# Reordered weight loads, other places for quarter weights and pinned casts at the stage borders of a one-core encoder step

## The chip, the core and the metric

The kernel runs on one core of one Trainium2 chip. Its metric is the device time of one execution, in microseconds (us). Three runs of the kernel before took 946.75, 948.52 and 948.81 us, with a median of 948.52.

The core has a matrix engine (TensorE, PE in the profile; its weight loads are a row of their own, PEld), an elementwise engine (VectorE, DVE), an activation and copy engine (ScalarE, ACT), GpSimd (POOL) and a sequencer that here only issues transfers (SyncE, SP). Each works through its own list of instructions in order. Transfers are issued by SP, by POOL and a few by ACT; 16 DMA engines carry them.

## The reference, cut to what matters

One layer over 2048 prompt frames and 32 new frames, with 1024 channels, in float32:

```python
hn = rmsnorm(h, g_mix)
proj = hn @ w_in                                   # 1024 x 3072
hA, bA, cA, zA, vB, zB = jnp.split(proj, [...], axis=-1)      # six parts of 512
yA, new_conv = short_conv_mixer(hA, bA, cA, zA, conv_hist, conv_w, conv_b)
yB, new_pool = pooling_mixer(vB, zB, pool_hist, pos, pool_w, pool_scale)
h = h + jnp.concatenate([yA, yB], axis=-1) @ w_out             # 1024 x 1024
gate = jax.nn.sigmoid(rmsnorm(h, g_ple) @ w_ple_gate)          # 1024 x 1024
h = h + (p @ w_ple) * gate                                     # p is 256 wide
return rmsnorm(h, g_final)
```

The states of the convolution and of the pooling are outputs too.

## The kernel before, in words

**How a product is made.** Every float32 factor is split in two: ScalarE casts the tile to a rounded part (`nc.scalar.copy`, the "cast" of the profile), VectorE subtracts that from the tile and keeps the rest (the "lo"). A product of two split factors takes three matmuls for each block of 128 (`FINE`, line 100). The big products are not made as eight quarter products but as seven, in the manner of Strassen and Winograd: `11`, `12·21`, `S2·T2`, `S1·T1`, `S3·T3`, `S4·22`, `22·T4`, each of 12 matmuls of 128x512. The names are those of the combined quarters: of the frames `11, 12, 22, S1..S4`, of the weights `11, 21, 22, T1..T4` (in the first stage the roles are exchanged). `seven` (line 249) writes the order of one pair of frame tiles; `step(1)` to `step(6)` in it are points where other work is put in. In its `late` form, used by the output stage, the order is 11, step 1, half of S1·T1, step 2, S2·T2, step 3, the other half, step 4, S3·T3, step 5, 12·21, S4·22, step 6, 22·T4.

**Stage 1, the input projection** (lines 375 to 1262), runs over two groups of 1024 frames and, in each, over four column blocks j. A unit (`Unit.seven`, line 963) has three pairs of kinds: zb with v, c with h, za with b. The frame pieces of the second group were stored to memory and are fetched by `load_group` (line 532): seven pieces of 2 MB, issued by POOL. The raw weights of a pair are two loads of 512 KB (`raw_weight`, line 546), issued by SP from `pair_weights` (line 568) in rows of 512 bytes; they have three places. In the first unit of the second group the first two pairs go side by side and the third begins (its loads too) after step 6 of the second, order list at lines 1036 to 1040. Beside the pairs runs `aside`: in the last three units of the second group it takes one step of `turn_p` (p is turned and split), `new_frames` (line 1080, the 32 new frames; it loads them, takes their mean square, normalizes them, turns them by matmul with the identity) and `ple_weights`, one step after each step of a pair.

**Stage 2, the output product** (lines 1353 to 1440), first makes the embedding p·w_ple of seven tiles (`embed`, line 140; `EARLY` = 7): 12 matmuls of 128x512 for each tile into two banks, ScalarE copies each bank (line 167), POOL stores the tile. Then it runs `seven` over eight pairs of tiles. Beside the embedding, the weights of `w_out` are split: upper rows `tops` (`wo_t`), lower rows `bots` (`wo_b`), parts by `weight_parts` (line 200) and `weight_part` (line 188: a subtraction for T1..T4, a cast, a lo). There are three big places (`acts`, `slot`, line 335) and one smaller (`seventh`, line 342). The quarters `11, T1` and `T2, T3` have one big place each, the embedding's output the third, and `22, 21` take that one later (`place_last`, line 1401); `T4` has the smaller place, which until then holds the p of tiles 2 to 6 (line 1366, five loads of 256 KB). `LATER` (line 1405) says which quarters are made at which step of the first pair. In the first pair the carries are ScalarE copies (line 1284), later VectorE adds (line 1279).

**Stage 3, the gate** (lines 1443 to 1735), makes the other tiles of the embedding, with w_ple loaded to `shared` (line 1452, four loads of 512 KB), and then runs `seven` over eight pairs; `prep_g` (line 1658) loads, turns and splits the frames of the next pair at steps 2 and 3. Odd tiles are turned by VectorE from four loads (`turned_here`, line 1481), even ones by TensorE from one load (`turned`, line 1467). Here `T2, T3` have a big place, `21` and `T4` follow in the two halves of `shared`, `22` has the smaller one (lines 1701 to 1711).

**What sets the order.** The program order is not the order on an engine. When the program is built, a planner walks through it with estimated times and lists each engine's instructions by when it takes them to be ready, earlier ones of the program first; the chip then runs each list in that order. `tc.keep_in_program_order(ins)` pins an instruction among those of its engine, `tc.issue_after(ins)` puts a block's instructions behind another one on that engine. The planner also gives each tile the first place of its pool that is free by its reckoning, and an instruction that writes a place waits until the earlier user is done.

Of the kernel before, what the change touches and what calls it, by code (L numbers as in the profile page):

```python
# [9 lines left out]
F32 = mybir.dt.float32  # L10
# [26 lines left out]
def trunk(ctx, tc, x_p, x_s, c_conv, c_pool, p_p, p_s, g_mix, w_in, conv_w, conv_b, pool_w,  # L37
# [150 lines left out]
    def weight_part(W, q, k, top, bot, ready=False):  # L188
# [5 lines left out]
        if x is not None and not ready:  # L194
            nc.vector.tensor_tensor(t, x, y, op=ALU.subtract)
        hi, lo = W[q][0][:, k], W[q][1][:, k]
        nc.scalar.copy(hi, t)
        return nc.vector.tensor_tensor(lo, t, hi.bitcast(F32), op=ALU.subtract)

    def weight_parts(W, tops, bots, *names):  # L200

        for q in names:
            for k in range(KH):
                ins = weight_part(W, q, k, tops[k], bots[k] if bots else None)
        return ins

    def frame_parts(cmb, tmp, name, a11, a12, a21, a22, between=None):
# [167 lines left out]
    with ExitStack() as s1:  # L375
# [156 lines left out]
        def load_group(g):  # L532
            B = six(g)
            B["T4"] = piece_of(seventh(f"B{g}_T4"), 0)
            for q in NAMES:
                nc.gpsimd.dma_start(B[q].bitcast(F32), p_d[q])
            return B
# [8 lines left out]
        def raw_weight(kind, j, name, ring=raw_ring):  # L546
            t = ring(f"raw_{name}")
            col = cols[kind] * WA + j * P
            raw_loads.append(nc.sync.dma_start(t, w_in[:, col:col + P].rearrange("(k p) n -> p k n", p=P)))
            return t  # L550

        raw_loads = []
# [527 lines left out]
        def new_frames():  # L1080
# [3 lines left out]
            yield  # L1084
            x = x_stat(x, True)
            yield
            normal(x)
            yield
# [175 lines left out]
    with ExitStack() as s2:  # L1264
# [44 lines left out]
        def prep_h(i, between=None):  # L1309
            lo, hi = load_y(i, 2 * P) if i else first_y  # L1310
            S[i], more = frame_parts(cmb, ss if i else None, f"y{i}", lo[:, :, :P], hi[:, :, :P], lo[:, :, P:], hi[:, :, P:],
                                     between)
# [33 lines left out]
        def rows_of_weight(pool, name, src, which):  # L1346
            a = []
            for k in range(KH):
# [15 lines left out]
        near = weight_seventh(W, "wo")  # L1364
        for i in range(2, EARLY):
            early_pps.append(load_pps(near[:, i * NH:i * NH + NH].rearrange("p (a k n) -> p a k n", a=2, k=2), i, nc.sync))
        bots, loaded = [], []

        def lower_rows():
            for k in reversed(range(KH)):  # L1370
                bots.insert(0, cmb.tile([P, D], F32, tag="c", name=f"wo_b_{k}"))
                last = (nc.sync if k < KH - 1 else nc.gpsimd).dma_start(bots[0], w_out[(KH + k) * P:(KH + k + 1) * P])
            loaded.append(last.ins)

        more = prep_h(0, lower_rows)
        weight_parts(W, tops, None, "11", "T1")
        weight_slot(W, "wo", *PLACES[1])
        space = acts[0].tile([P, SLOT], F32, tag="hn", name="eouts")
# [5 lines left out]
        for c in range(EARLY):  # L1384
            run(c)
# [3 lines left out]
        weight_parts(W, tops, bots, "T2")  # L1389
# [11 lines left out]
        def place_last():  # L1401
            weight_slot(W, "wo", *PLACES[2])
            later("21", 0)()

        LATER = {1: later("T3"), 2: place_last, 3: later("22", 1), 4: later("T4", 2)}
# [12 lines left out]
        for i in range(0, NT - 1, 2):  # L1418
# [19 lines left out]
            if i == 0:  # L1438
                next_gate()
                nc.sync.dma_start(g_bc, g_fin.partition_broadcast(P))  # L1440
# [8 lines left out]
        got = {c: load_pps(st.tile([P, 2, 2, P], F32R, tag="t", name=f"pps_{EARLY + c}"), EARLY + c, nc.sync) for c in range(2)}  # L1449
        for k in range(2):  # L1450
            for h in range(2):
                nc.sync.dma_start(wp[k][h].bitcast(F32), wl_d[k][h])
        bots, _ = rows_of_weight(cmb, "wg_b", g_d, 1)
# [27 lines left out]
        def turned_here(i):  # L1481
# [3 lines left out]
            for q in range(4):  # L1485
                nc.sync.dma_start(t[q * 32:q * 32 + 32].rearrange("p (g c) -> p g c", g=4),
                                  h_d[r:r + P, q * 256:q * 256 + 256].rearrange("(g p) c -> p g c", p=32))
            nc.vector.transpose(t, t)
# [169 lines left out]
        def prep_g(i):  # L1658
# [105 lines left out]
```

## Time and profile before

| What | Value |
|---|---|
| median of three runs | 948.52 us |
| the profiled execution | 950.14 us |
| its span, first to last instruction | 948.3 us |
| PE / PEld busy | 911.1 / 728.1 us |
| DVE / ACT / POOL busy | 696.5 / 457.4 / 150.3 us |
| mean granted clock of TensorE | 0.985 |
| moved by DMA | 199.57 MB, 210 GB/s over the span |

Stage 1 fills the span up to 545 us, stage 2 goes from there to 734 us, stage 3 to the end. A row of the timeline gives start, length, engine, line, operation, output and inputs, shape and count, and in brackets the idle time of the engine in front of it and what ended it. Since matmuls are pipelined, a row of 12 is shown some 0.16 us longer than the distance to the next row.

### The profile page before, as it was taken

The page shows a single profiled execution, that of the slowest core. Times are in us where ns is not written, and L with a number is a line of the kernel's source. Part 1 is how long each engine was busy: PE and PEld are TensorE (multiplying, and loading weights), DVE is VectorE, ACT ScalarE, POOL GpSimd, SP SyncE. Part 2 cuts the span into 40 slices and gives each one's busy share as a digit, 9 for nine tenths or more (in the row PEclk, how much of TensorE's full clock was granted, in tenths as well). Part 3 has the DMA queues.
Part 4 walks back from the last instruction along what each step waited for, and adds up shares of the span by engine and source line. Part 5 has one row for each costly group of instructions (what it writes and reads, how often), then busy time and mean ns, then how long its engine had stood idle before and what let it go on. Part 6 is the DMA issues. An engine that isn't in the chain of part 4 may idle for free. (4 is left out here: it accounts for less than half of the span.)

```text
span 948.3 us, 12212 instructions
## 1 busy us (share of the span) xinstructions
PE 911.1 (96%) x4186; PEld 728.1 (77%) x4186; DVE 696.5 (73%) x1148; ACT 457.4 (48%) x828; POOL 150.3 (16%) x291
## 2 busy tenths in 40 slices
PE   8999999999999899999999988999999999999996
PEld 6788887778887688666688866878887778877885
DVE  6995888797982597746677668855655858899884
ACT  7752554455443344423343356624435755565553
POOL 2200121122121014100010021211111301111112
PEclk9999999999999899999999999999999899999999
DMA  8165295756699556687652565876777794656563
GB/s 270 47 203 191 78 289 166 225 165 202 192 363 406 117 189 207 209 277 223 204 182 89 188 258 201 247 242 225 230 241 264 276 259 164 190 193 222 194 195 133
DMA packets 115099, 199.57 MB, mean 210 GB/s; under 512 B 13270, under 2 KB 72062, under 8 KB 114013
## 3 DMA queue, kind: packets, MB, share of 16 engines
q1 hardware_dynamic: 93181, 126.63, 42.9%
q0 software_dynamic: 19408, 67.77, 21.1%
q10 hardware_dynamic: 2448, 4.39, 1.3%
q8 instruction: 33, 0.54, 0.2%
q14 instruction: 29, 0.24, 0.1%
HBM read 133.06 MB, written 65.67 MB: 210 GB/s over the span
## 5 line engine op out<-in xcount | busy, mean ns | idle before, releaser
L185 PE MATMUL x_o<-wo_T,y_S 128*128 128x512 f32 x192 | 46.4, 391 | 2.9 <-ACT c_o L1284 2.9
L185 PE MATMUL z_g<-wg,g_S 128*128 128x512 f32 x192 | 48.5, 398 | 0.0
L185 PE MATMUL z_o<-wo,y_S 128*128 128x512 f32 x192 | 47.6, 390 | 0.0
L185 PE MATMUL x_g<-wg_T,g_S 128*128 128x512 f32 x192 | 46.9, 391 | 0.0
L185 PEld LDWEIGHTS x_o<-wo_T,y_S 128*128 128x128 f32 x192 | 35.9, 188 | 11.1 <-ACT c_o L1284 3.7
L185 PEld LDWEIGHTS z_g<-wg,g_S 128*128 128x128 f32 x192 | 36.4, 192 | 7.6 <-ACT c_g L1499 0.2
L185 PEld LDWEIGHTS x_g<-wg_T,g_S 128*128 128x128 f32 x192 | 36.2, 188 | 7.6
L615 PE MATMUL z_ch<-B,w_ch_S 128*128 128x512 f32 x168 | 40.8, 392 | 1.2 <-ACT U L935 1.2
L185 PEld LDWEIGHTS z_o<-wo,y_S 128*128 128x128 f32 x192 | 36.0, 188 | 7.7 <-DVE y_S L84 0.3
L615 PE MATMUL x_ch<-B,w_ch_S 128*128 128x512 f32 x168 | 41.8, 392 | 0.0
L615 PE MATMUL x_zab<-B,w_zab_S 128*128 128x512 f32 x168 | 41.4, 394 | 0.4 <-ACT V L935 0.4
L615 PE MATMUL z_zab<-B,w_zab_S 128*128 128x512 f32 x168 | 41.7, 396 | 0.0
L615 PE MATMUL z_zbv<-B,w_zbv_S 128*128 128x512 f32 x168 | 41.5, 397 | 0.0
L615 PE MATMUL x_zbv<-B,w_zbv_S 128*128 128x512 f32 x168 | 40.6, 391 | 0.0
L615 PEld LDWEIGHTS z_ch<-B,w_ch_S 128*128 128x128 f32 x168 | 31.3, 188 | 8.9 <-ACT U L935 1.6
L615 PEld LDWEIGHTS z_zbv<-B,w_zbv_S 128*128 128x128 f32 x168 | 32.0, 192 | 7.5 <-issue 0.8
L615 PEld LDWEIGHTS x_zab<-B,w_zab_S 128*128 128x128 f32 x168 | 31.4, 189 | 8.4 <-issue 1.2
L615 PEld LDWEIGHTS z_zab<-B,w_zab_S 128*128 128x128 f32 x168 | 31.6, 190 | 7.4 <-issue 1.0
L615 PEld LDWEIGHTS x_zbv<-B,w_zbv_S 128*128 128x128 f32 x168 | 31.4, 188 | 7.3 <-issue 0.8
L615 PEld LDWEIGHTS x_ch<-B,w_ch_S 128*128 128x128 f32 x168 | 31.3, 188 | 7.3 <-issue 0.8
L1518 DVE SCALAR_TENSOR_TENSOR h<-h,rstd_f,g_bc 128x1024 f32<-128x1024 f32 (+1 forms) x15 | 19.2, 1283 | 15.4 <-POOL rstd_f L77 15.2
L81 ACT CAST y_S<-y_fS 128x512 fp32r<-128x512 f32 x28 | 17.1, 619 | 25.3 <-PE x_o L185 11.6
(562 smaller groups left out, 2303.0 us busy)
## 6 DMA issues: line engine op xcount, KB each, us to landing
wn<-in_w_in_dram SPq DMA_DIRECT2D x24, 512.0 KB, 4.8
p_dT<-T POOLq DMA_DIRECT2D x16, 512.0 KB, 5.1
y<-y_d SPq DMA_DIRECT2D x16, 512.0 KB, 4.5
h<-h_d SPq DMA_DIRECT2D x16, 512.0 KB, 5.8
e<-e_d SPq DMA_DIRECT2D x15, 512.0 KB, 4.7
x<-in_x_prompt_dram SPq DMA_DIRECT2D x14, 512.0 KB, 4.5
out_dram<-h POOLq DMA_DIRECT2D x14, 512.0 KB, 3.7
B<-p_d POOLq DMA_DIRECT2D x3, 2048.0 KB, 16.3
```

The lines of the kernel that those rows point to most:

```text
L81: ins = nc.scalar.copy(hi, src)
L185: nc.tensor.matmul(ps[:n], lhs[:, k, a, :n], w[b][:, k], start=start and k + q == 0, stop=k == KH - 1 and q == 2, skip_group_check=True)
L615: nc.tensor.matmul(ps, lhs[:, k, x], b[:, k, y], start=start and k + q == 0, stop=stop and k == KH - 1 and q == 2, skip_group_check=True)
L1518: nc.vector.scalar_tensor_tensor(h[:n], h[:n], rf[:n], g_bc[:n], op0=ALU.mult, op1=ALU.mult)
```

## The change

1. **Third pair of the second group's first unit.** `load_group` now also issues three raw weights, right behind its seven pieces: those of zb on SP, those of za and b on POOL. `raw_weight` hands them out when the pair asks for them.
2. **New frames.** `new_frames` has three more empty steps: one between load and mean square, one between that and the normalization, one behind it.
3. **Output weights.** The place of the embedding's output (`space`) is taken before that of `T2, T3`. The p of tiles 2 to 6 come by one load into the half place of T3. `21` has the smaller place, `22, T4` a big one. T2 is made ahead of the sixth tile of the embedding, in the row order 2, 1, 0, 3. The subtractions and casts of T2, T3, 21 and 22 are pinned. 21 and 22 are both made at step 2 of the first pair. Three lower rows of the weights are loaded behind the first split of the first frames, the fourth behind the second one.
4. **Final gain.** `g_bc` is loaded in the second pair (i = 2), not in the first.
5. **Gate weights.** One p tile instead of two and two lower rows instead of four are loaded ahead of w_ple, the other two rows behind it. `21, 22` have the big place, `T3` the smaller one, `T2` and `T4` the halves of `shared`.
6. **Gate frames.** The frames of the second gate pair are loaded ahead of h and e of the first, and that h is issued by POOL.

```diff
@@ weight_part, weight_parts @@
-        if x is not None and not ready:
-            nc.vector.tensor_tensor(t, x, y, op=ALU.subtract)
+        if x is not None and not ready:
+            ins = nc.vector.tensor_tensor(t, x, y, op=ALU.subtract)
+            if pin:
+                tc.keep_in_program_order(ins)
         hi, lo = W[q][0][:, k], W[q][1][:, k]
-        nc.scalar.copy(hi, t)
+        ins = nc.scalar.copy(hi, t)
+        if pin:
+            tc.keep_in_program_order(ins)
@@ frame_parts @@
             put("11", a11)
-            between()
+            between[0]()
             put("S3", comb("S3", a11, a21, ALU.subtract, a11))
+            between[1]()
@@ load_group, raw_weight @@
+            for kind, name, queue in (("zb", "zbv", nc.sync), ("za", "zab", nc.gpsimd), ("b", "zab", nc.gpsimd)):
+                name = f"{name}_{g}_0{'b' if kind == 'b' else 'a'}"
+                raw_ahead[name] = raw_weight(kind, 0, name, queue=queue)
...
+            if name in raw_ahead:
+                return raw_ahead.pop(name)
@@ stage 2 @@
-        near = weight_seventh(W, "wo")
-        for i in range(2, EARLY):
-            early_pps.append(load_pps(near[...], i, nc.sync))
+        space = acts[0].tile([P, SLOT], F32, tag="hn", name="eouts")
+        pair = weight_slot(W, "wo", *PLACES[1])[:, SLOT // 2:SLOT // 2 + (EARLY - 2) * NH]
+        with tc.issue_after(last_raw):
+            nc.sync.dma_start(pair.rearrange("p (i n) -> p i n", n=NH).bitcast(F32),
+                              pp_d[2:EARLY].rearrange("i p n -> p i n"))
...
+        W["21"] = halves(seventh("wo_21"))
...
         for c in range(EARLY):
+            if c == EARLY - 2:
+                weight_parts(W, tops, bots, "T2", order=(2, 1, 0, 3), pin=True)
             run(c)
...
-        weight_parts(W, tops, bots, "T2")
...
+        def third():
+            hold.append(weight_parts(W, tops, bots, "T3", pin=True))
+
+        def left():
+            weight_parts(W, tops, bots, "21", pin=True)
+            weight_slot(W, "wo", "22", "T4")
+            hold.append(weight_parts(W, tops, bots, "22", pin=True))
+            more(0)
+
+        LATER = {1: third, 2: left, 3: later(1), 4: later("T4", 2)}
@@ stage 3 @@
+        got = {0: load_pps(st.tile(...), EARLY, nc.sync)}
+        head, _ = rows_of_weight(cmb, "wg_b", g_d, 1, (0, 1))
         for k in range(2):
             for h in range(2):
-                nc.sync.dma_start(wp[k][h].bitcast(F32), wl_d[k][h])
+                last_q = nc.sync.dma_start(wp[k][h].bitcast(F32), wl_d[k][h])
-        bots, _ = rows_of_weight(cmb, "wg_b", g_d, 1)
+        bots = head
+        with tc.issue_after(last_q.ins):
+            bots += rows_of_weight(cmb, "wg_b", g_d, 1, (2, 3))[0]
...
+        W["T2"] = halves(shared)[2:]
+        weight_parts(W, tops, bots, "T2")
+        W["T3"] = halves(seventh("wg_T3"))
+        weight_parts(W, tops, bots, "T3")
+        weight_slot(W, "wg", "21", "22")
+        weight_parts(W, tops, bots, "21", "22")
...
-            h = [load_rows(xh, "h", i + b, h_d) for b in range(2)]
+            following = prep_g(i + 2, not i)
+            h = [load_rows(xh, "h", i + b, h_d, queue=nc.sync if i else nc.gpsimd) for b in range(2)]
```

More of the change, by code (lines that the diff above doesn't have):

```diff
@@ L1344, in scale_gate, with rows_of_weight @@
             return rest
-        def rows_of_weight(pool, name, src, which):
+        def rows_of_weight(pool, name, src, which, ks=range(KH)):
             a = []
-            for k in range(KH):
+            for k in ks:
                 a.append(ring4(pool, f"{name}_{k}") if pool is not cmb else cmb.tile([P, D], F32, tag="c", name=f"{name}_{k}"))
@@ L1439, in trunk @@
                 next_gate()
-                nc.sync.dma_start(g_bc, g_fin.partition_broadcast(P))
+            if i == 2:
+                with tc.issue_after(summed[-1].ins):
+                    nc.sync.dma_start(g_bc, g_fin.partition_broadcast(P))
         W = {}
@@ L1479, in turned, with by_quarters @@
             return out
-        def turned_here(i):
+        def by_quarters(i):
             r, n = tiles[i]
@@ L1672, in prep_g, with load @@
             lower = []
+            def load():
+                got["lower"] = by_quarters(i + 1)
+                got["upper"] = load_rows(ya, "hn", i, h_d) if i else first_h
+            if ahead:
+                load()
             def first():
-                lower.extend(turned_here(i + 1))
+                if not ahead:
+                    load()
+                lower.extend(turned_here(got["lower"]))
             def second():
```

61 lines of the change are left out of this document (28 added, 33 removed).

## The prediction

> **What bounds the kernel now.** I read the page's first part, then the waits of PE, then PE's timeline, and at each of its holes the timeline of the engine or queue that PE waited for.
>
> ```profile
> PE 911.1 (96%) x4186; PEld 728.1 (77%) x4186; DVE 696.5 (73%) x1148; ACT 457.4 (48%) x828; POOL 150.3 (16%) x291
> ...
> PE x_zab L615 <- ACT w_zab L81: 6.2, 1, 6.2
> PE e L109 <- ACT eouts L167: 3.5, 1, 3.5
> PE x_o L185 <- ACT c_o L1284: 2.9, 2, 2.2
> PE e L109 <- DMA wq<-wl_d: 2.7, 3, 1.5
> PE pth L1477 <- ACT ho L1475: 2.1, 1, 2.1
> PE pt_new L1092 <- DVE xt_new L453: 1.4, 1, 1.4
> PE x_o L185 <- DVE x L1279: 0.8, 1, 0.8
> ```
>
> PE is busy for 911.1 of 948.3 us. The change takes no matmul away, so it can only win in the 37.2 us in which PE stands, and in what a stop costs behind it. Seven rows of waits, 19.6 us in all, lie at the places that the diff touches. The waits are not the whole loss, since the clock falls in them:
>
> ```profile
> 312.70:322.20 9.50, 9.47 (x34) 7.65 (x35) 3.39 (x7) 1.13 (x2) 0.00 (x0) 0.79 0.81 180
> 396.70:408.00 11.30, 11.27 (x62) 6.96 (x62) 4.41 (x7) 2.09 (x4) 0.00 (x0) 0.85 0.87 264
> 780.40:786.00 5.60, 5.55 (x22) 4.64 (x23) 4.07 (x7) 3.35 (x6) 0.00 (x0) 0.70 0.45 139
> ```
>
> The third number from the end is the granted clock: 0.79, 0.85 and 0.70 behind waits of 6.2, 1.4 and 2.1 us. So I price each hole by distances in the timeline against a full rate, waits and slow matmuls together. The full rate comes from two rows that follow each other: 12 matmuls in 303.64 - 300.92 = 2.72 us, 0.2267 each.
>
> ```profile
> 300.92 2.88 PE L615 MATMUL x_zbv<-B,w_zbv_S 128*128 128x512 f32 x12
> 303.64 2.88 PE L615 MATMUL x_ch<-B,w_ch_S 128*128 128x512 f32 x12
> 312.73 2.50 PE L615 MATMUL x_zab<-B,w_zab 128*128 128x512 f32 x5 [6.21 <-ACT w_zab L81]
> 322.15 2.20 PE L615 MATMUL x_zbv<-B_T,w_zbv 128*128 128x512 f32 x9
> ```
>
> **1, the third pair.** PE was free at 303.64 + 2.72 = 306.36. Up to 322.15 it made 33 matmuls (5 and 4 of zab, two S4 products of 12), 7.48 us; lost: 8.3. PE's list held zab's first product in front of the two S4 products, and zab's raw weights were late:
>
> ```profile
> raw_zab_0b<-in_w_in_dram SPq DMA_DIRECT2D x1, 512.0 KB, 48.7
> raw_zbv_0b<-in_w_in_dram SPq DMA_DIRECT2D x1, 512.0 KB, 4.1
> B_T<-p_dT4b POOLq DMA_DIRECT2D x1, 2048.0 KB, 30.7
> 279.62 0.53 POOL L536 DMA_DIRECT2D B_T<-p_dT4b  x1 [1.67 <-PE x_zab L615]
> 312.06 1.14 ACT L81 CAST w_zab<-raw_zab_0a 128x512 fp32r<-128x512 f32 x2 [9.84 <-DMA raw_zab_0a<-in_w_in_dram]
> ```
>
> The same 512 KB take 4.1 us alone, but 48.7 us (the second) beside the seven pieces of the other queue, whose last lands at 279.62 + 30.7 = 310.3. Behind the pieces on POOL's queue, both raws land by 310.3 + 2 x 4.1 = 318.5 at the latest, the first by 314.4; at the earliest by some 306 and 308, as the pieces share with nothing. That helps PE little in itself: what counts is the list. The planner put zab first since it took the raws to be there before the last pieces; in one queue behind the last piece they can't be. So I expect both S4 and both 22 products first: 306.36 + 4 x 2.72 = 317.2 for zab's first product (first raw at 314.4 at worst, two casts of 0.6 us), and two products later, at 322.7, for the first that needs the second raw. Both bounds fit. What is late next is the last piece, wanted at 306.36 + 2 x 2.72 = 311.8 and there at 310.3 in before, so 1.5 us ahead. I take **7.3 of 8.3**; ends 8.3, and 0 if the list keeps its order. The three POOL issues and the one of SP stand in front of nothing that PE awaits: SP's raw of zb is issued early in before too, POOL's next loads (p) are for the next unit.
>
> The Trainium skill's "DMA: Bandwidth & Descriptors" (Issuing engines are not separate DMA queues) says that the issuing engine saves issue time only, the same 16 engines carrying all. By that rule the move to POOL would win nothing; the 4.1 against 48.7 speaks for the place in the queues.
>
> **2, the new frames.** A wait of 1.4 us, then 11.3 us at clock 0.85 (second window above): 1.4 + 0.15 x 11.3 = 3.1. Three empty steps of one product each give the chain of load, mean square, scale and transpose 8.2 us more, against a wait of 1.4; behind it only the same part's later steps move, and the three units have 72 steps where the parts take 49 and now 52. I take **2.5**; ends 0 (the planner puts the transposes as early as it did) and 3.1.
>
> **3, the output stage up to its first product.**
>
> ```profile
> 545.01 5.73 PE L109 MATMUL e<-wp,pps 128*128 128x512 f32 x24
> 569.58 2.88 PE L185 MATMUL x_o<-wo,y 128*128 128x512 f32 x12
> 560.54 0.69 DVE L195 TENSOR_TENSOR wo_t<-wo_b,wo_t 128x512 f32<-128x512 f32 x1 [5.88 <-DMA wo_b<-in_w_out_dram]
> 561.26 0.62 ACT L197 CAST wo_T<-wo_t 128x512 fp32r<-128x512 f32 x1 [5.95 <-DVE wo_t L195]
> wo_T<-pp_d SPq DMA_DIRECT2D x5, 256.0 KB, 3.1
> g_bc<-in_g_final_dram SPq DMA_DIRECT2D x1, 512.0 KB, 11.0
> 555.00:557.50 2.50, 2.50 (x13) 2.07 (x12) 0.00 (x0) 0.31 (x1) 0.00 (x0) 1.00 1.03 419
> ```
>
> 84 embedding matmuls from 545.01 are 19.04 us, to 564.05; the first product began at 569.58: 5.5 lost. The cause stands in three rows: a lower weight row landed at 560.5, VectorE's T2 waited for it, and ScalarE's T2 cast waited in front of the copies that PE needed to reuse its banks. Two parts of the change meet it. The pin keeps the T2 casts behind the copies of the first five tiles, so at 545.01 + 10 x 1.36 = 558.6 ScalarE has freed ten banks, and PE can go on over six banks, 8.2 us, without the next copy. And 5 x 256 KB of p go out before 545 (T3's place is free when the S4·22 product of the last pair has read it) and 512 KB of g_bc much later: 1.8 MB less at 419 GB/s, 4.3 us sooner for the rows. Either alone would do. I take the whole **5.5**, with 3 as the low end for an order of casts that I don't see.
>
> **4, the first output pair.**
>
> ```profile
> 593.68 2.43 PE L185 MATMUL x_o<-wo,y 128*128 128x512 f32 x10
> 577.35 3.22 ACT L197 CAST wo<-wo_b 128x512 fp32r<-128x512 f32 x6 [2.35 <-DMA e_d<-eouts]
> 580.48 0.57 ACT L1284 COPY c_o<-x_o 128x512 f32<-128x512 f32 x1
> ```
>
> From 569.58 to 593.68 PE made 86 matmuls (84 and 2 of the next pair), 19.5 us; lost: 4.6, most of it behind the copy c_o at 580.48, which stood behind six casts that had waited 2.35 us for a store of the embedding. In the change 21 needs no such store. But T3 can be cast only behind the last embedding product (564.05, as p lies in its place) and, pinned behind the first carry copy, from 564.05 + 2.72 + 0.57 = 567.4; with four casts each of T3, 21 and 22 at 3.22 / 6 = 0.54 us the queue of 12 ends at 573.8, and if the second carry stands behind it, at 574.4. S3·T3 wants that copy at 564.05 + 3 x 2.72 = 572.2. So one wait of 2.2 us stays where 4.6 was lost. VectorE also has less time to catch up. I take **1.7**; ends 4.6 (the copy is put ahead of 22) and -2.5 (22's casts still wait for the store, rival B).
>
> **5, the gate's embedding.**
>
> ```profile
> 731.34 2.88 PE L185 MATMUL x_o<-wo_T,y 128*128 128x512 f32 x12
> 753.90 1.03 PE L1477 MATMUL pth<-ident,ho 128*128 128x128 f32 x8
> 730.02 0.32 SPq L129 DMA_DIRECT2D pps<-pp_d  x1
> 730.46 2.01 SPq L1452 DMA_DIRECT2D wq<-wl_d  x4
> 723.18 2.88 PE L185 MATMUL x_o<-wo_T,y_S 128*128 128x512 f32 x12
> ```
>
> PE was free at 734.06; five tiles are 60 matmuls, 13.6 us, to 747.7; the transposes came at 753.90: 6.2 lost. The w_ple loads stood in SP's queue behind a p tile at 730.02, which is no longer in front. Their place is that of `T2, T3`, free after the product at 723.18 + 2.72 = 725.9, so they go out 4.5 us earlier, behind 1 MB less; the last wait ended at 738.6, and 4.5 less is 734.1, just when PE wants the first. I take **4.5**, a short wait being left; ends 2 and 6.2. The quarters behind it: 21 is wanted first and can now be made early; T2, wanted one product (2.72 us) later, takes over the place that frees last, so the order of needs is better than before.
>
> **6, the second gate pair's frames.**
>
> ```profile
> 775.70 2.65 PE L185 MATMUL x_g<-wg_T,g_S 128*128 128x512 f32 x11
> 785.97 2.88 PE L185 MATMUL x_g<-wg,g 128*128 128x512 f32 x12
> 769.02 1.97 SPq L1486 DMA_DIRECT2D hn<-h_d  x4
> 764.79 2.90 PE L185 MATMUL x_g<-wg,g 128*128 128x512 f32 x12
> ```
>
> 24 matmuls and 8 transposes (1.03) are 6.5 us; PE took 785.97 - 775.70 = 10.3: 3.8 lost. The frames' loads went out at 769.02, 4.2 us after the end of the embedding at 764.79. In the change they stand first, but their places are those of the upper weight rows, which T2 now holds until its lo: cast 0.6, lo 0.7, so from 766.2 on, 2.8 us sooner, and without h in front. The wait was 2.1, so it goes. e and h come later and can hold VectorE. I take **3.0**; ends 0 and 3.8.
>
> The Trainium skill's page "TensorE: Matmul & The Clock Gate" (What's actually happening) has the clock fall only after an idle window of about 3.4 us; by that rule 2, 5 and 6 could win their waits alone, 1.4, 2.7 and 2.1, and the sum would be 3.8 us smaller. The third window, clock 0.70 behind a wait of 2.1 us, disagrees, and the rows decide.
>
> **Sum:** 7.3 + 2.5 + 5.5 + 1.7 + 4.5 + 3.0 = 24.5 us. The profiled execution took 950.14 (span 948.3 and 1.84 around it), so 925.6 by it; it is 1.62 above the median of the runs shown, so the median comes to 948.52 - 24.5 = **924.0**.
>
> **Rivals.**
>
> A, the queue changes nothing for PE: the planner still lists zab's product first. For it: the list follows estimates that were 40 us wrong in before. Then PE waits from 306.36 for a raw at 308 to 314.4: as long as before, within some 4 us. 924.0 + 7.3 = **931**. Chance 0.17. (The rule of the Trainium skill's DMA page on issuing engines, cited above, points this way.)
>
> B, the pins hold the carry copies: 22's casts, pinned in front of the second carry, wait for the embedding's last store as those at 577.35 did, S3·T3 with them. Price: 2.5 lost instead of 1.7 won, **928**. Against it: copies and store come earlier, as ScalarE isn't blocked at 561. Chance 0.17.
>
> C, slower: VectorE's backlog of the first output pair never drains, and each of the seven later pairs waits as pair 2 of the gate does, 3.8 us: 924.0 + 7 x 3.8 = **951**. It decides from the point at which VectorE has more than the 19.04 us of a pair to do. Against it:
>
> ```profile
> 657.90:676.94 19.04, 19.04 (x86) 15.77 (x85) 10.75 (x17) 7.21 (x12) 4.32 (x8) 1.00 0.73 234
> ```
>
> VectorE is busy for 10.75 us of such a pair. Chance 0.07.
>
> **How the numbers follow.** The forecast has 0.56, with its own range 917 (all 31.5 us won) to 930. The 0.03 left lies between it and before. A and B together are 935.5, with 6's gain gone too 938.5: range 917 to 939. A measurement of this kernel can tell about 0.2% (1.9 us) from no change. Faster 0.56 + 0.17 + 0.17 = 0.90; same 0.03; slower 0.07.
>
> **What would show it.** 1: z_zbv follows S3·T3 without a hole at 306 and x_zab comes after the 22 products. 2: no wait of pt_new. 3: the first product of the output at 564 minus what was won before it, no wait of e for eouts. 4: one wait of x_o for c_o, about 2 us. 5: w_ple issued right behind the last S3·T3. 6: no wait of pth for ho. I would be wrong if a hole moves to the next late thing: the last frame piece, 22's casts, or e in the gate's first pair.

## The result and the profile after

The changed kernel took 938.75 us (median of four runs, 936.91 to 940.55), the kernel before 948.66 beside it (four runs, 946.75 to 950.83): ratio 0.9895, 95% interval 0.9861 to 0.9928, 9.9 us less. The forecast was 924.0, so of the 24.5 us it promised, 10 came. The profiled execution took 940.35 us with a span of 938.3, against 948.3 before. The first part of its page, busy times by engine:

```profile
PE 909.1 (97%) x4186; PEld 727.1 (77%) x4186; DVE 698.1 (74%) x1148; ACT 459.0 (49%) x828; POOL 149.7 (16%) x295
```

PE stands for 29.2 us now, 37.2 before. The waits of PE say where (total, times, longest):

```profile
PE x_o L185 <- ACT wo L199: 3.1, 1, 3.1
...
PE e L109 <- DMA wq<-wl_d: 2.0, 1, 2.0
PE pth L1506 <- ACT ho L1504: 2.0, 1, 2.0
...
PE x_zab L625 <- ACT w_zab_S L81: 1.4, 1, 1.4
...
PE z_zab L625 <- ACT w_zab_S L81: 0.8, 1, 0.8
```

Six of the seven old rows at the places of the change are gone from there; e for w_ple is still there with 2.0 us. New are the first, the third (in a later gate pair than before) and the last two. So holes were closed and others opened. Which counts most is read from distances between stages on PE's timeline, waits and slow clock together:

| Stretch of PE's timeline | before, us | after, us | won | forecast |
|---|---|---|---|---|
| start to first embedding product, parts 1 and 2 | 545.01 | 536.20 | 8.8 | 9.8 |
| embedding, to the first output product, part 3 | 24.57 | 19.16 | 5.4 | 5.5 |
| first two output pairs | 42.85 | 47.86 | **-5.0** | **1.7** |
| other output pairs, to PE free for the gate | 121.63 | 122.70 | -1.1 | 0 |
| embedding of the gate, part 5 | 30.73 | 28.59 | 2.1 | 4.5 |
| first gate pair (72 matmuls) with the next frames, part 6 | 21.18 | 17.29 | 3.9 | 3.0 |
| rest | 162.3 | 166.5 | **-4.2** | 0 |

The sum before rounding is 10.0, the difference of the spans. Three rows of seven are right; the output pairs miss 6.7 us, the rest of the gate 4.2, its embedding 2.4. Each column is one profile, and the runs below show how far a row moves from one to the next.

**The first output pair.** PE's timeline:

```profile
536.20 5.73 PE L109 MATMUL e<-wp,pps 128*128 128x512 f32 x24
...
555.36 2.88 PE L185 MATMUL x_o<-wo,y 128*128 128x512 f32 x12
...
566.78 0.50 PE L185 MATMUL x_o<-wo_T,y_S 128*128 128x512 f32 x1 [0.52 <-ACT wo_T L199]
...
577.66 8.13 PE L185 MATMUL x_o<-wo,y 128*128 128x512 f32 x22 [3.12 <-ACT wo L199]
```

The embedding runs without a hole now (19.16 us for 84 products). But the last product of the pair, 22·T4, waits 3.1 us for T4's cast, and the 22 matmuls in that row (12 of it, ten of the next pair) take 8.1 us where 22 x 0.2267 are 5.0: the third number from the end of the next row, the granted clock, is 0.62.

```profile
567.80:577.60 9.80, 6.60 (x27) 4.91 (x27) 9.80 (x18) 6.06 (x11) 0.00 (x0) 0.97 0.54 169
577.60:585.80 8.20, 8.13 (x22) 6.13 (x22) 4.94 (x9) 2.99 (x6) 2.70 (x6) 0.62 0.77 238
```

In the first of these windows VectorE (the third pair of numbers) is busy 9.80 us of 9.80. Why it was so late shows on its timeline from T2's first subtraction on:

```profile
550.67 0.68 DVE L195 TENSOR_TENSOR wo_t<-wo_b,wo_t 128x512 f32<-128x512 f32 x1
...
554.03 0.69 DVE L202 TENSOR_TENSOR wo_T<-wo_t,wo_T 128x512 fp32r<-128x512 f32 x1 [0.69 <-ACT wo_T L199]
554.63 0.69 DVE L195 TENSOR_TENSOR wo_t<-wo_b,wo_t 128x512 f32<-128x512 f32 x1
556.01 0.69 DVE L202 TENSOR_TENSOR wo_T<-wo_t,wo_T 128x512 fp32r<-128x512 f32 x1 [0.69 <-ACT wo_T L199]
...
567.20 0.68 DVE L202 TENSOR_TENSOR wo_T<-wo_t,wo_T 128x512 fp32r<-128x512 f32 x1
567.80 4.90 DVE L202 TENSOR_TENSOR wo<-wo_b,wo 128x512 fp32r<-128x512 f32 x8
```

and on ScalarE's:

```profile
561.72 0.62 ACT L199 CAST wo_T<-wo_t 128x512 fp32r<-128x512 f32 x1 [1.79 <-DVE wo_t L195]
...
566.63 4.26 ACT L199 CAST wo<-wo_b 128x512 fp32r<-128x512 f32 x8
...
576.95 0.62 ACT L199 CAST wo<-wo_b 128x512 fp32r<-128x512 f32 x1 [1.79 <-DVE wo_b L195]
```

Subtraction (L195), cast (L199), lo (L202), next subtraction: one part at a time, each engine waiting for the other. The eight parts of T2 and T3 take from 550.67 to 567.88, 17.2 us, 2.15 a part. Only then come 21, 22 and T4.

**The rest of the gate.** SyncE's queue in the third gate pair:

```profile
796.87 1.75 SPq L1515 DMA_DIRECT2D hn<-h_d  x4
804.30 0.34 SPq L377 DMA_DIRECT2D h<-h_d  x1
804.68 0.43 SPq L377 DMA_DIRECT2D hn<-h_d  x1
```

and ScalarE, for which PE's transposes then wait 2.0 us:

```profile
811.43 1.14 ACT L1504 COPY ho<-hn 128x512 f32<-128x512 f32 x2 [4.10 <-DMA hn<-h_d]
```

The frame row hn stands behind an h row that went out only at 804.30, when its place came free. In the kernel before both h rows of that pair had gone out together at 800.19, well ahead of the frames at 815.31, so hn had no waiting row in front of it.

**The third pair.** S4 and 22 come first, without a hole, as forecast. But what comes next on PE waits:

```profile
308.94 2.88 PE L625 MATMUL z_ch<-B,w_ch_S 128*128 128x512 f32 x12
...
317.10 2.88 PE L625 MATMUL x_zab<-B,w_zab 128*128 128x512 f32 x12
...
324.73 0.74 PE L625 MATMUL x_zab<-B,w_zab_S 128*128 128x512 f32 x2 [1.35 <-ACT w_zab_S L81]
326.30 0.73 PE L625 MATMUL z_zab<-B,w_zab_S 128*128 128x512 f32 x2 [0.83 <-ACT w_zab_S L81]
```

since VectorE takes S2's subtraction (the L587 row) behind operations of another chain, four of them 2.73 us in all:

```profile
320.09 2.73 DVE L1080 SCALAR_TENSOR_TENSOR c_s<-U,vec,c_s 128x512 f32<-128x512 f32 x4
322.75 0.68 DVE L1072 SCALAR_TENSOR_TENSOR pl<-win,V 128x512 f32<-128x512 f32 x1
323.35 0.68 DVE L587 TENSOR_TENSOR raw_zab_0a<-s_zab,raw_zab_0a 128x512 f32<-128x512 f32 x1
```

At the same number of matmuls PE is 8.45 us ahead of before at 314 us, and 5.7 us ahead at 328.

### The profile page after: what moved, and what is told of

Same layout as the page of the kernel before. It is cut to its first block, busy times and chain, and to the rows that moved or that the text cites. A ratio compares the mean times of both kernels' runs of the same rounds, so it can differ in the third digit from the quotient of the medians.

```text
span 938.3 us, 12210 instructions
## 1 busy us (share of the span) xinstructions
PE 909.1 (97%) x4186; PEld 727.1 (77%) x4186; DVE 698.1 (74%) x1148; ACT 459.0 (49%) x828; POOL 149.7 (16%) x295
## 4 chain that ended last, share of the span: by engine, by line
PE 64%; DVE 5%; DMA 5%; ACT 2%; issue 2%; POOL 1%; POOLq 0%; SPq 0%; DVEq 0%; ACTq 0%
PE x_g L185 8%; PE x_zab L625 7%; PE x_o L185 6%; PE x_ch L625 6%; PE x_zbv L625 5%; PE e L109 4%; PE z_g L185 4%; PE z_zab L625 4%; PE z_ch L625 3%; PE z_o L185 3%; PE z_zbv L625 2%; PE y_g L185 2%; PE y_zab L625 1%; PE y_o L185 1%; PE new L1124 1%
## 5 line engine op out<-in xcount | busy, mean ns | idle before, releaser
L185 PE MATMUL x_o<-wo,y 128*128 128x512 f32 x192 | 48.3, 407 | 3.1 <-ACT wo L199 3.1
L185 PEld LDWEIGHTS x_o<-wo,y 128*128 128x128 f32 x192 | 38.0, 199 | 11.9 <-ACT wo L199 3.5
L1551 DVE SCALAR_TENSOR_TENSOR h<-h,rstd_f,g_bc 128x1024 f32<-128x1024 f32 (+1 forms) x15 | 19.2, 1280 | 12.7 <-POOL rstd_f L77 12.0
```

The source lines that it names most:

```text
L185: nc.tensor.matmul(ps[:n], lhs[:, k, a, :n], w[b][:, k], start=start and k + q == 0, stop=k == KH - 1 and q == 2, skip_group_check=True)
L1551: nc.vector.scalar_tensor_tensor(h[:n], h[:n], rf[:n], g_bc[:n], op0=ALU.mult, op1=ALU.mult)
```

## The experiments

Theory T: the pins on subtraction *and* cast chain each part of T2 and T3 over two engines, and T4 is late. R1: not the pins, but that 22 is made ahead of T4. Q: the rest of the gate is lost to the order of one queue.

### No pins, cast pins, 22 later

Without pins:

```diff
-weight_parts(W, tops, bots, "T2", order=(2, 1, 0, 3), pin=True)
+weight_parts(W, tops, bots, "T2", order=(2, 1, 0, 3))
```

and so for T3, 21 and 22.

> The changed kernel with no pin on T2, T3, 21 and 22. Theory T (the pins chain subtraction, cast and lo of each part of T2 and T3, 2.0 to 2.3 us a part instead of about 1.45, so that T4's casts are 3.1 us late): VectorE makes the eight parts of T2 and T3 at about 1.4 us each, the wait of x_o for wo's cast in 22*T4 goes, and the first two output pairs (first product to first product of the third pair) fall from 47.9 to 42 to 45 us; the whole is 13 to 16 us under the kernel before instead of 9.9. A wait of x_o for the carry copy c_o of up to 2.2 us may come back, since nothing holds the casts behind it. Rival R1 (not the pins: 22 made ahead of T4 at step 2, in place of step 3): 47 to 49 us for the two pairs, 9 to 11 us under the kernel before.

Measured: 940.17 us, ratio 0.9921 (0.9893 to 0.9948), no faster than the changed kernel; the two pairs 46.6 us, the embedding 22.1 instead of 19.2. Its waits of PE:

```profile
PE x_o L185 <- ACT c_o L1297: 4.1, 2, 3.2
PE e L109 <- ACT eouts L167: 2.7, 1, 2.7
```

The chain is gone, but the planner again puts casts in front of the copies that free PE's banks, those of the embedding (2.7) and the carries (3.2). The pins on the casts do what the prediction said of them. So this run cannot settle T; the next one does. Only the casts pinned:

```diff
             ins = nc.vector.tensor_tensor(t, x, y, op=ALU.subtract)
-            if pin:
-                tc.keep_in_program_order(ins)
```

> The changed kernel with the casts pinned and the subtractions not. T: the chain is broken as well, since VectorE may run its subtractions ahead in threes; the two pairs take 42 to 45 us, within 1.5 us of the kernel without any pin. If the pinned casts alone were the cause: 47 to 49 us, as in the changed kernel. R1: 47 to 49 us.

Measured: 934.0 us, ratio 0.9857 (0.9837 to 0.9878); the two pairs **42.5** us instead of 47.9, the embedding 19.17 as in the changed kernel. VectorE's timeline:

```profile
551.94 1.89 DVE L195 TENSOR_TENSOR wo_t<-wo_b,wo_t 128x512 f32<-128x512 f32 x3
553.75 1.89 DVE L202 TENSOR_TENSOR wo_T<-wo_t,wo_T 128x512 fp32r<-128x512 f32 x3
555.55 1.90 DVE L195 TENSOR_TENSOR wo_t<-wo_b,wo_t 128x512 f32<-128x512 f32 x3
...
560.78 2.49 DVE L202 TENSOR_TENSOR wo_T<-wo_t,wo_T 128x512 fp32r<-128x512 f32 x4
```

Three subtractions run, then three lo's: T2 and T3 take 551.94 to 563.27, 11.3 us instead of 17.2. T is confirmed at its place. In time the median is 4.7 us under the changed kernel's 938.75, and 2.3 under the 936.32 that it took in a later set of runs; two more profiles with this edit, below, have 42.5 and 44.1 us in the two pairs. That the kernel without any pin would be as fast was wrong. A smaller wait is left, y_o for the frame part 12, whose cast now stands behind 22's:

```profile
566.94 0.74 PE L185 MATMUL y_o<-wo,y 128*128 128x512 f32 x2 [2.00 <-ACT y L81]
```

22 made at step 3, all pins kept:

```diff
-            hold.append(weight_parts(W, tops, bots, "22", pin=True))
             more(0)
+        def late_22():
+            hold.append(weight_parts(W, tops, bots, "22", pin=True))
+            more(1)
```

> The changed kernel, pins kept, with 22 made at step 3 as in the kernel before, and not at step 2. T: the chain of T2 and T3 is the same, so T4's casts stay late, and the two pairs take 46.5 to 49 us (47.9 in the changed kernel). R1: 42 to 45 us, and the wait of 22*T4 for the cast goes.

Measured: 935.31 us, ratio 0.9875 (0.9854 to 0.9895); the two pairs 46.0 us, between the two forecasts. The wait of 22·T4 is still there, now for a sum that stands behind T4's work on VectorE:

```profile
PE x_o L185 <- DVE x L1292: 3.8, 1, 3.8
```

So R1 holds for 1.9 of the 5.4 us at most: casts and lo's of 21 and 22 fill holes of the chain. Of the 1.9, 1.3 lie in the clock: the 22 matmuls behind the wait took 6.83 us here and 8.13 in the changed kernel. Most of the rest of this run's lead over the changed kernel lies in the gate's embedding (26.3 us for 28.6).

### The output stage as before

The text of the output stage from before (places, p loads, quarters, no pins) in the changed kernel:

```diff
-        LATER = {1: third, 2: left, 3: later(1), 4: later("T4", 2)}
+        LATER = {1: later("T3"), 2: place_last, 3: later("22", 1), 4: later("T4", 2)}
```

> The changed kernel with the output stage's quarters, places, p loads and pins as in the kernel before (part 3 undone; parts 1, 2, 4, 5 and 6 stay). The prediction gave part 3 and its first output pair 7.2 us, so this would be 945 to 947 us. Theory T (5.4 us won up to the first product are lost again in the first two output pairs, 5.0 us): within 1.5 us of the changed kernel, 937.5 to 940.5 us, with the first product 5 us later behind the embedding's start, and the two pairs 5 us shorter.

Measured: 937.08 us, ratio 0.9865 (0.9817 to 0.9914). The embedding takes 24.46 us, 5.3 more than with the change, the two pairs 42.65, 5.2 less. What part 3 wins up to the first product, its pins lose in the first pair; the 7.2 us of the forecast are not there.

### Part 1 alone, and its queue

The three raw loads in the kernel before, nothing else:

```diff
+            for kind, name, queue in (("zb", "zbv", nc.sync), ("za", "zab", nc.gpsimd), ("b", "zab", nc.gpsimd)):
+                raw_ahead[name] = raw_weight(kind, 0, name, queue=queue)
```

> The kernel before with part 1 of the change alone (three raw weights issued behind the seven pieces). The prediction: 7.3 us less, no wait of x_zab for w_zab, the S4 and 22 products ahead of zab's first product. What the changed kernel showed: 8.45 us ahead after the S4 products, 2.8 of them given back in waits of 1.4 and 0.8 us for w_zab_S about 18 us later. If that loss belongs to part 1, this kernel shows it too and is 5 to 7 us faster than before; if it comes from another part, 7 to 8.5.

Measured: 939.14 us, ratio 0.9891 (0.9868 to 0.9914): as fast as the whole change, and with 9.7 us outside both forecasts of the time (5 to 7 and 7 to 8.5). In the profile it is 9.2 us ahead behind the S4 products and 6.4 at 327 us (0.9 of each is there at 300 us already), so the 2.75 us of loss belong to part 1. At the start of the embedding it leads by 8.6: another 2.2 us were won behind 327 us, without part 2, though PE still waits 0.9 us for the new frames. The rest of its lead lies behind that, where the kernel is the one before, so it is spread between profiles.

The same two raws issued by SP, in the changed kernel:

```diff
-("za", "zab", nc.gpsimd), ("b", "zab", nc.gpsimd)):
+("za", "zab", nc.sync), ("b", "zab", nc.sync)):
```

> The changed kernel with the two raw weights of za and b issued by SP, at the same place in the program, and not behind the pieces on POOL's queue. Theory (the place behind the pieces in one queue decides, through the landing time and the list): the raws take 40 to 50 us beside the pieces (48.7 in the kernel before, 31 in the changed one), five zab products stand in front of the S4 product again and wait, and the embedding starts 5 to 9 us later than at 536.2. Rival (the early issue alone decides, the queue does not matter): landings within 5 us of the changed kernel, and the embedding's start within 1.5 us of 536.2.

Measured: 943.89 us, ratio 0.9942 (0.9907 to 0.9977); the embedding starts at 542.04, 5.8 us later than in the changed kernel's first profile and 4.3 later than in its second (537.70). The hole is back on PE:

```profile
312.09 2.50 PE L625 MATMUL x_zab<-B,w_zab 128*128 128x512 f32 x5 [6.01 <-ACT w_zab L81]
```

and of the DMA issues the second raw landed after 48.0 us, where behind the pieces (the second line, changed kernel) it took 32.2:

```profile
raw_zab_0b<-in_w_in_dram SPq DMA_DIRECT2D x1, 512.0 KB, 48.0
raw_zab_0b<-in_w_in_dram POOLq DMA_DIRECT2D x1, 512.0 KB, 32.2
```

These are times from the issue, and SP issued 12 us earlier. What counts is when the raws landed, and that hardly moved. The first cast waits for the first raw here, and POOL's next load does so in the changed kernel:

```profile
311.42 1.14 ACT L81 CAST w_zab<-raw_zab_0a 128x512 fp32r<-128x512 f32 x2 [9.64 <-DMA raw_zab_0a<-in_w_in_dram]
311.35 0.65 POOL L1194 DMA_DIRECT2D p<-in_p_prompt_dram  x1 [1.41 <-DMA raw_zab_0a<-in_w_in_dram]
```

So the first raw is there at 311.4 or 311.3, whichever engine issues it; the second lands at 269.09 + 48.0 = 317.1 against 281.48 + 32.2 = 313.7. Both are within the 5 us of the rival. The queue still decides the time, but through PE's list alone: zab's first product stands in front of the S4 products again, and PE waits for a raw that comes when it did in the changed kernel. The Trainium skill's "DMA: Bandwidth & Descriptors" (Issuing engines are not separate DMA queues) says that another issuing engine saves issue time only; the two landings of the first raw agree with it, and the 5.8 us come from the order that the planner makes, not from the transfers.

### The h row

```diff
-            h = [load_rows(xh, "h", i + b, h_d, ...) for b in range(2)]
+            h = [load_rows(xh, "h", i + b, h_d, ...) for b in range(1 if i == 4 else 2)]
+            if i == 4:
+                first = following[2]
+                following[2] = lambda: (first(), h.append(load_rows(xh, "h", 5, h_d)))
```

> The changed kernel with one load moved: in the third gate pair the second h row goes out behind the frames of the next pair, not ahead of them. Theory Q (a queue runs in order, so the frame row waited behind an h row whose place came free at 804.3 us): the wait of pth for ho of 2.0 us goes, and from the end of the first gate pair to the end of the span it takes 162 to 164 us instead of 166.5; the whole 2 to 4 us less than the changed kernel, 12 to 14 under the kernel before. Rival (the frame row is late because the transfers themselves are): the wait stays within 1 us of 2.0, and so does the time.

Measured: 935.53 us, ratio 0.9869 (0.9835 to 0.9902). SyncE's queue:

```profile
794.84 0.91 SPq L1515 DMA_DIRECT2D hn<-h_d  x2
796.13 0.34 SPq L377 DMA_DIRECT2D hn<-h_d  x1
801.51 6.08 SPq L377 DMA_DIRECT2D h<-h_d  x2
```

hn goes out at 796.13, ahead of the h row; PE's wait for ho is gone, and the stretch from the end of the first gate pair is 163.4 us instead of 166.5. The difference of medians, 3.2 us, lies within the two kernels' spread; the wait and the distance carry the verdict. Over all runs of this document that stretch is 164.1 to 166.8 us in the eight profiles with the h row ahead of the frames and 163.4 to 163.9 in the five with it behind, so Q is confirmed.

### The loads in front of the gate

```diff
-        head, _ = rows_of_weight(cmb, "wg_b", g_d, 1, (0, 1))
...
+            bots += rows_of_weight(cmb, "wg_b", g_d, 1)[0]
```

All four rows behind w_ple.

> The changed kernel with the two lower rows of the gate's weights behind w_ple and not ahead of it (1 MB less in front). Theory (w_ple is late since the queue ahead is still moving those rows: 11 us from issue to the last landing instead of 8): w_ple is issued within 1 us of 718, lands 2 to 3 us sooner, the wait of e for w_ple (0.9 to 2.0 us in the runs so far) goes, and the embedding of the gate takes 25 to 27 us instead of 28.6. Rival (other traffic, stores and the quarters of hn, sets it): the landing stays at 10 to 11 us behind the issue. The price to watch is T2, whose lower rows come later: a wait of the first gate pair for a cast of wq or of wg_T up to 2 us.

Measured: 940.75 us, ratio 0.9908 (0.9873 to 0.9943); the gate's embedding 30.5 us. The wait for w_ple is gone and a longer one is there, for a p tile:

```profile
PE e L109 <- DMA pps<-pp_d: 4.0, 1, 4.0
```

With two p tiles between w_ple and the rows, and with cast pins and the h row as above:

```diff
+            got[1] = load_pps(st.tile(...), EARLY + 1, nc.sync)
+            got[2] = load_pps(st.tile(...), EARLY + 2, nc.sync)
```

> The changed kernel with casts pinned and subtractions not, the h row of the third gate pair behind the next frames, and in front of the gate the loads in the order of need: w_ple, two more p tiles, then the four lower rows (the run with the rows straight behind w_ple waited 4.0 us for a p tile behind them). Theory (one queue, in order, at a rate that leaves no slack): no wait of e for w_ple or a p tile over 1 us, the gate's embedding takes 24.8 to 26 us; 927 to 931 us in all. Rival (the bytes themselves are too many before 735 us, in whatever order): some load still comes late by 2 us or more, and the embedding takes 27 us or more; 931 to 934.

Measured: 933.12 us, ratio 0.9832 (0.9779 to 0.9884); embedding of the gate 29.35 us, and

```profile
PE e L109 <- DMA pps<-pp_d: 2.9, 1, 2.9
```

The forecast of the rival came: in every order some load comes late. That it is the bytes in front of the gate that are too many fits the DMA engines, busy for the whole of 725 to 735 us in the changed kernel and in both of these (share 1.00 to 1.02), but no run took bytes away. Two rows ahead, as the change has it, was the best of the orders tried.

### Combinations

The first one had cast pins, h row, w_ple first, and the frame part 12 split ahead of T3:

```diff
+            more(0)
             hold.append(weight_parts(W, tops, bots, "T3", pin=True))
```

> The changed kernel with four edits: casts pinned and subtractions not (4.7 us less on medians), the h row of the third gate pair behind the next frames (2.5 to 3.4 less), w_ple ahead of the lower rows of the gate's weights (1 to 3 less), and the frame part 12 of the first output pair split ahead of T3 instead of behind 22, so that y_o does not wait 2.0 us for its cast. If they add up: 926 to 930 us, 18 to 22 us under the kernel before, and the first two output pairs take 40 to 42 us. If they hide one another: 931 to 934.

Measured: 934.37 us, ratio 0.9833 (0.9811 to 0.9854), 14.5 us under the kernel before. The wait for part 12 is gone, one of 2.4 us for a sum of VectorE comes in its place, and w_ple first costs a p tile's wait of 2.7. They hide one another. VectorE ran from 551.64 to 578.62 with a single pause of 0.31 us, so I tried to take work from it:

```diff
-        return nc.vector.tensor_tensor(lo, t, hi.bitcast(F32), op=ALU.subtract)
+        return (nc.gpsimd if pin and q == "22" else nc.vector).tensor_tensor(...)
```

> The changed kernel with casts pinned and subtractions not, the h row as above, and the four lo's of 22 on GpSimd. Theory V (with the chain gone VectorE itself is the bound of the first output pair: 44 operations of 0.60 us without a gap from the first T2 subtraction on, 26.5 us, where TensorE has 19 us of products): VectorE ends the pair 2.4 us sooner, and the first two pairs take 1 to 2.4 us less than with the casts pinned alone; 929 to 931.5 us in all. Rival (GpSimd's slower operation, 1.3 us for its one row of this size, makes 22 late): S4*22 waits for GpSimd's lo, and the two pairs take as long or up to 2 us longer.

Measured: 936.24 us, ratio 0.986 (0.9803 to 0.9918), the two pairs 44.15 us: no gain. The first two of GpSimd's four subtractions:

```profile
564.02 9.14 POOL L202 TENSOR_TENSOR wo<-wo_b,wo 128x512 fp32r<-128x512 f32 x1 [6.66 <-ACT wo L199]
573.14 1.29 POOL L202 TENSOR_TENSOR wo<-wo_b,wo 128x512 fp32r<-128x512 f32 x1
```

The first took 9.14 us, the other three 1.27 to 1.71, and the last ended at 577.34, so S4·22 waited for 22. The run cannot show whether VectorE was the bound. Last, the two edits that had won, the changed kernel again, and the changed kernel with the gate's stage from before, five runs each, beside eleven of the kernel before (median 947.57).

```diff
-            following = prep_g(i + 2, not i)
+            seven(f"g{i}", A, W, *gate_ops(h, e, P, f"g{i}", i), prep_g(i + 2))
```

is one line of the third edit, which undoes parts 5 and 6.

> The changed kernel once more, for its spread and as the mate of the other two. In six kernels with the same order of loads in front of the gate the gate's embedding took 25.3 to 26.9 us, in the one profile of the changed kernel 28.6. If that is the run's own spread, this profile shows 25.5 to 27.5 us there, with a wait of e for w_ple of 0.7 to 1.5 us, and the first two output pairs again 47.8 us and the wait of pth for ho 2.0 us; 937 to 940 us in all. If it belongs to the kernel: 28 us or more.

> The changed kernel with the two edits that proved themselves: casts pinned and subtractions not, and the h row of the third gate pair behind the next frames. If they add up (5.4 us in the first two output pairs, 3.0 behind the second gate pair): 929 to 932 us, 7 to 9 us under the changed kernel of the same job. If one hides the other: 933 to 935.

> The changed kernel with the gate's stage as in the kernel before (parts 5 and 6 undone; parts 1 to 4 stay). By the prediction, 4.5 + 3.0 = 7.5 us slower than the changed kernel. By the profiles so far the gate's start and first pair win about 4.5 to 7 us and the h row ahead of the frames gives 3.0 back, so 1.5 to 4.5 us slower than the changed kernel of the same job, and without the wait of pth for ho in the second gate pair. If the gate's parts won nothing: within 1 us.

| Kernel | median us (range) | ratio to before | first two output pairs | gate's embedding | from the end of the first gate pair |
|---|---|---|---|---|---|
| changed, again | 936.32 (934.75 to 939.68) | 0.9899 (0.987 to 0.9929) | 47.0 | 25.7 | 164.9 |
| cast pins and h row | **930.47** (929.7 to 931.28) | 0.9835 (0.9805 to 0.9865) | 44.1 | 27.0 | 163.5 |
| gate as before | 937.71 (936.36 to 937.91) | 0.9908 (0.9881 to 0.9934) | 47.9 | 28.9 | 163.1 |

The two mended causes add up to the time that was forecast, 929 to 932, and 17.1 us less than the kernel before. Against the changed kernel beside it they win 5.9 us, less than the 7 to 9 forecast: that kernel was itself 2.4 us faster than in its first set, and the two output pairs fell by 2.9 us instead of 5.4, 1.6 of it because the clock fell here behind the wait that is left in them (last section). The changed kernel's second profile has 25.7 us in the gate's embedding, so the 28.6 of the first were that run's. Its two output pairs take 47.0 us and the wait of pth is 2.0 again: these belong to the kernel. Parts 5 and 6 together bring 1.4 us in medians, with overlapping ranges, where 7.5 were forecast; in these two profiles they win 3.2 in the gate's embedding and 1.7 in the first gate pair, and then give back 1.7 behind it, where the h row stands.

## Why the prediction was wrong

The direction was right, and the terms 1 (7.3 forecast, 5.7 measured) and 3 (5.5, 5.4) stand. For term 2 (2.5) the first profile has 3.1, but 2.2 of it came without part 2 in the run with part 1 alone, so no more than 0.9 is shown to be its own. Terms 5 (4.5) and 6 (3.0) came to 2.1 and 3.9 in the first profile and to 5.1 and 3.9 in the second, all against one profile of the kernel before. Over all runs the gate's embedding took 28.9 to 30.7 us in the three profiles with the gate of before and 25.3 to 28.6 in the ten with the change's loads, the first gate pair 18.6 to 21.2 and 17.2 to 18.5. The means differ by 3.3 and 1.9 us: both terms have the right sign and are smaller than forecast.

**The step that failed is 4, the first output pair.** It said that "with four casts each of T3, 21 and 22 at 3.22 / 6 = 0.54 us the queue of 12 ends at 573.8", 9.8 us behind the first product, that one wait of 2.2 us for a carry copy stays, and took 1.7 us of gain. The queue ended at 570.89, 15.5 us behind the first product at 555.36; 5.0 us were lost. I had priced the casts alone, back to back on ScalarE. But the diff pins the subtractions too, and a part of T3 is subtraction, cast and lo on two engines: in program order each next subtraction stands behind the lo that waits for the cast, 2.15 us a part. With the subtractions free the queue of 12 is

```profile
560.03 2.18 ACT L199 CAST wo_T<-wo_t 128x512 fp32r<-128x512 f32 x4
562.12 4.26 ACT L199 CAST wo<-wo_b 128x512 fp32r<-128x512 f32 x8
```

so it begins 3.40 us behind that run's first product at 556.63 and ends at 566.38, 9.75 us behind it: both numbers as forecast, so ScalarE's price was right and the chain was missing. T4 behind the queue was not in the step either, and that is where PE waited, not at a carry copy. The sentence "VectorE also has less time to catch up" named the engine and gave it no price.

**The second miss is that the rest of the gate was taken as unchanged.** Part 6 was costed for the first pair only. With parts 5 and 6 an h row that waits for its place came to stand ahead of the frames of a later pair; the run with both undone does not have that wait. Which of the two parts brings it, and why the place comes free late, is not shown. It cost 4.2 us in the first profile and 2.5 in the second; moving the h row alone cures 3.1 and 1.4 of that.

Term 1 lost 1.6 of its 7.3 at "what is late next": I looked at the frame pieces, which came in time, and not at VectorE, whose S2 subtraction stood behind another chain. That is read from the trace; a run that moves this subtraction was not made.

The rivals: A fell, the list changed as forecast, with zab's first product at 317.10 where 317.2 was forecast, and the run with the raws on SP shows that the issuing queue changes the list. That 4.1 against 48.7 us speaks for the place in the queues, as the prediction has it, the landings do not bear out. B fell, no cast waited for the embedding's store. C was half right: VectorE's backlog is real, 9.80 us busy of 9.80, but it stays in the first pair, and the later ones lose 1.1 us in sum in the first profile and nothing in the second (121.6 us). The cause that came was none of the three: a pin that orders more than it is meant to.

## What to carry to other kernels

Price a pinned or hand-ordered instruction with everything that then stands behind it on its engine: if the steps of one item run on two engines, ordering all of them serializes the items, and ordering only the one that must not overtake is enough. After such a change compare the order on every engine and queue to the end of the program, not only at the place of the edit. And add up stages: a change that wins 8.8 us in one and loses 5.0 in the next shows as one small number.

## What was not expected of the hardware

- **The same wait costs a different clock.** With cast pins PE waits 2.00 us in the same place in two runs; the granted clock (third from the end) behind it is 1.00 with the cast pins alone,

```profile
565.00:572.00 7.00, 5.06 (x22) 4.10 (x23) 7.00 (x13) 5.97 (x12) 0.00 (x0) 1.00 0.22 56
```

and 0.76 with the h row moved as well:

```profile
563.50:570.50 7.00, 5.18 (x16) 4.04 (x17) 6.57 (x11) 4.45 (x10) 0.00 (x0) 0.76 0.25 68
```

There 12 matmuls took 4.4 us instead of 2.8, 1.6 us of difference, where the two kernels differ only in one load of the gate. The changed kernel's own two profiles show it with no difference at all: behind the same 2.00 us wait of pth the clock is 0.76 in the first (810 to 817 us) and 1.00 in the second (806.6 to 813.6). The Trainium skill's "TensorE: Matmul & The Clock Gate" (What's actually happening) says that the activity window is free-running, so that the moment of a change depends on where in the window the work lands; it says so of the start of a kernel, and both pairs of profiles fit it here, though no run shows the window itself. Its table has the clock fall after an idle window of some 3.4 us or more; that does not agree, since it fell behind waits of 2.00 us.

- **GpSimd beside a busy VectorE.** The first of its four subtractions of 128x512 began at 564.02, while VectorE ran without a pause, and ended at 573.16, 1.1 us after VectorE's first pause began (572.03). The other three took 1.27 to 1.71 us, as long as the one row of that size elsewhere in the changed kernel, a product:

```profile
L1605 POOL TENSOR_TENSOR hg<-h,g_bc 128x512 f32<-128x512 f32 x1 | 1.3, 1297 | 0.1
```

Beside them two operations of VectorE took 1.55 and 1.76 us instead of 0.69. This fits two engines that hold each other up; it is one profile, in which the spans of GpSimd are rough, and no run here was made to test it.

- **One profile carries several us.** The kernel before ran from 942.24 to 954.14 us in eleven runs, the changed one from 934.75 to 939.68 in five, the version with both mended causes from 929.7 to 931.28. One execution of the first lies up to 6.6 us from its median, and a term of 4 us read from one profile carries that.
